# A third pair of K-blocks as seven products of sums in the feed-forward of a decoder layer

## Chip, cores and metric

The kernel runs on one core of a Trainium2 chip. The metric is the device time of one execution in microseconds (us), as the median of several runs. The program is one launch and every engine (TensorE, here PE; VectorE, DVE; ScalarE, ACT; GpSimd, POOL; SyncE, SP, which issues the weight loads) works through its own queue in order, with semaphores between them.

## The reference

One decoder layer over 256 tokens of width 2048, in float32: a norm, a token mixer with its input and output projections, a second norm, and a gated feed-forward with 5632 hidden columns. The part that matters here is this one:

```python
h = rms_norm(x, pre_ffn_g[l])
f = (jax.nn.silu(h @ w_gate[l]) * (h @ w_up[l])) @ w_down[l]
x = x + rms_norm(f, post_ffn_g[l])
```

## The kernel before

**Precision.** Each float32 operand is held as a rounded high part (hi) and the rest (lo), both in a 32-bit matmul type. A product is three matmuls into one PSUM bank: hi times hi, lo times hi, hi times lo (L664 to L666 in the joint chunks; the stationary side is a 128x128 block of activations, the moving side 128x512 weights). The weights come from memory in float32 as `raw` tiles of two K-blocks by 512 columns (512 KB). For a tile in plain use ACT makes hi (L79) and DVE makes lo = raw - hi (L81).

**Chunks.** The hidden columns are cut into 11 chunks of 512. Chunk 0 and chunks 9 and 10 are done gate first, then up. Chunks 1 to 8 (`gate_up`, L716) take gate and up together: the 16 K-blocks (128 rows each) are gone through as 8 pairs, p = 0 to 7. For one pair the operands are 2x2 blocks on both sides: two token blocks by two K-blocks of activations, and two K-blocks by two column chunks (gate, up) of weights.

**Two ways for a pair.** A plain pair ("P", `plain_pair`, L611) is eight products into four banks: four with the gate tile, then four with the up tile. A pair in `S_PAIRS` ("S", `seven_products`, L619) is seven products of sums into seven banks (Winograd's form): the sums of activation blocks are made once (`x1_sums`, L711, `token_sums`, L577); the sums of weight blocks are made anew for every chunk on DVE, in place in the raw tiles (L627 to L629 three, L635 one), and are split into hi (ACT, L623, L624, L634, L636) and lo (DVE, L605, four times). PE's order in an S pair is: two products with `h1`, one with `h22` (the tile `m`), two with `h3` (`hi_sb`), two with `h2` (`hi_sa`). Before the change S_PAIRS is (2, 5).

**After the last S pair** of a chunk (p = 5) one copy on ACT (L672) and four additions on DVE (L673 to L676) bring four of the seven banks together in `comb`. After pair 7 DVE adds the plain banks (L743 for gate, L750 for up), ACT takes the tanh (L745), DVE multiplies (L746, L695). The rows are transposed on PE (L687) at the end of pair 1 of the next chunk, and DVE and ACT take them out of PSUM (L690, L691).

**Buffers.** There are four raw tiles (`wraw`, L64), so the load for pair p+2 goes into a tile that pair p gives back. SP's queue issues the loads (L77 for plain pairs, L601 for S pairs), in order, two for each pair. There are five hi and five lo tiles (`wsplit`, L61); a plain pair takes two of each, an S pair three. `m22` (tag h9, one buffer) holds `h22` and `l22` of an S pair. The tag h10 (one buffer) holds the temporary of the activation sums, and later `comb`.

**Order.** The order of each engine's queue is not the source order: it is fixed when the program is put together, by what can run and by source order among that, and is the same in each execution. So work of one chunk and of the next stands mixed in DVE's and ACT's queues, as the rows below show.

Of the kernel before, what the change touches and what calls it, by code (L numbers as in the profile page):

```python
# [9 lines left out]
F32R = mybir.dt.float32r  # L10
# [4 lines left out]
P = 128  # L15
# [18 lines left out]
def trunk(  # L34
# [123 lines left out]
    with ExitStack() as mctx:  # L158
# [318 lines left out]
        x1_of = lambda kb: (x1_hi[:, kb], x1_lo[:, kb])  # L477
# [77 lines left out]
    hpool = ctx.enter_context(tc.tile_pool(name="hpool", bufs=1, side="right"))  # L555
    gctx = actx.enter_context(ExitStack())
    gu = gctx.enter_context(tc.tile_pool(name="gu", bufs=1))
# [17 lines left out]
    sums = {}  # L575

    def token_sums(key, pairs, hi, lo, tmp, home):  # L577

        n = pairs * 512
        a = tmp[:, 0].rearrange("p (q e t) -> p q e t", q=pairs, e=2)  # L580
        f = tmp[:, 1].rearrange("p (q s t) -> p q s t", q=pairs, s=4)
        nc.vector.tensor_tensor(out=tmp[:, 0].rearrange("p (k t) -> p k t", k=2 * pairs), in0=hi.bitcast(F32),
                                in1=lo.bitcast(F32), op=ALU.add)
        a11, a21 = a[:, :, 0, TB[0]], a[:, :, 0, TB[1]]
        a12, a22 = a[:, :, 1, TB[0]], a[:, :, 1, TB[1]]
        nc.vector.scalar_tensor_tensor(out=f[:, :, 0], in0=a21, scalar=-1.0, in1=a22, op0=ALU.mult, op1=ALU.subtract)
        nc.vector.scalar_tensor_tensor(out=f[:, :, 1], in0=f[:, :, 0], scalar=-1.0, in1=a11, op0=ALU.mult,
                                       op1=ALU.subtract)
        nc.vector.tensor_tensor(out=f[:, :, 2], in0=a11, in1=a21, op=ALU.subtract)
        nc.vector.tensor_tensor(out=f[:, :, 3], in0=a12, in1=f[:, :, 1], op=ALU.subtract)  # L590
        flat = tmp[:, 1]
        s_hi = home[:, 0].rearrange("p q s t -> p (q s t)")
        s_lo = home[:, 1].rearrange("p q s t -> p (q s t)")
        nc.scalar.copy(out=s_hi, in_=flat)
        nc.vector.tensor_tensor(out=s_lo, in0=flat, in1=s_hi.bitcast(F32), op=ALU.subtract)
        for q in range(pairs):
            sums[key, q] = [(home[:, 0, q, j], home[:, 1, q, j]) for j in range(4)]

    def fetch(piece):
        raw = wraw.tile([P, 2, 512], F32, tag="raw", name="raw")  # L600
        nc.sync.dma_start(out=raw, in_=piece)  # L601
        return raw

    def lo_of(lo, raw, hi):
        nc.vector.tensor_tensor(out=lo, in0=raw, in1=hi.bitcast(F32), op=ALU.subtract)  # L605

    def block(act_of, kb, tb):
        hi, lo = act_of(kb)
        return hi[:, TB[tb]], lo[:, TB[tb]]

    def plain_pair(srcs, p, act_of):  # L611

        out = []
        for src, banks in zip(srcs, ((1, 3), (2, 7))):
            hi, lo = split_weights(src[p], 2, 512)
            out.append([(banks[tb], block(act_of, 2 * p + e, tb), (hi[:, e], lo[:, e])) for e in range(2) for tb in range(NT)])
        return out

    def seven_products(srcs, p, act_of, s_of, h22, l22):  # L619
        ra, rb = (fetch(src[p]) for src in srcs)  # L620
        h1 = wsplit.tile([P, 2, 512], F32R, tag="hi", name="hi")
        l1 = wsplit.tile([P, 2, 512], F32R, tag="lo", name="lo")
        nc.scalar.copy(out=h1, in_=ra)  # L623
        nc.scalar.copy(out=h22, in_=rb[:, 1])  # L624
        lo_of(l1, ra, h1)
        lo_of(l22, rb[:, 1], h22)
        for out, in0, in1, op in ((ra[:, 0], ra[:, 0], rb[:, 0], ALU.subtract), (rb[:, 0], rb[:, 1], rb[:, 0], ALU.subtract),  # L627
                                  (rb[:, 1], rb[:, 1], ra[:, 0], ALU.add)):
            nc.vector.tensor_tensor(out=out, in0=in0, in1=in1, op=op)  # L629
        h2 = wsplit.tile([P, 2, 512], F32R, tag="hi", name="hi_sa")  # L630
        l2 = wsplit.tile([P, 2, 512], F32R, tag="lo", name="lo_sa")
        h3 = wsplit.tile([P, 2, 512], F32R, tag="hi", name="hi_sb")
        l3 = wsplit.tile([P, 2, 512], F32R, tag="lo", name="lo_sb")
        nc.scalar.copy(out=h3, in_=rb)  # L634
        nc.vector.tensor_tensor(out=ra[:, 1], in0=ra[:, 1], in1=rb[:, 1], op=ALU.subtract)  # L635
        nc.scalar.copy(out=h2, in_=ra)  # L636
        lo_of(l3, rb, h3)
        lo_of(l2, ra, h2)
        s1n, s2, s3, s4 = s_of
        return [[(0, block(act_of, 2 * p, 0), (h1[:, 0], l1[:, 0])),  # L640
                 (1, block(act_of, 2 * p + 1, 0), (h1[:, 1], l1[:, 1])),
                 (2, s4, (h22, l22))],
                [(6, s3, (h3[:, 0], l3[:, 0])),
                 (5, s2, (h3[:, 1], l3[:, 1]))],
                [(4, s1n, (h2[:, 0], l2[:, 0])),
                 (3, block(act_of, 2 * p + 1, 1), (h2[:, 1], l2[:, 1]))]]
# [3 lines left out]
    def products_into(kinds, new_bank):  # L650

        left = {}
        for k in kinds:
            for b, n in (PLAIN if k == "P" else tuple((b, 1) for b in range(7))):
                left[b] = left.get(b, 0) + n
        banks = {}

        def product(b, a, w):
            start = b not in banks
            if start:  # L660
                banks[b] = new_bank(b)
            left[b] -= 1
            (a_hi, a_lo), (w_hi, w_lo) = a, w
            nc.tensor.matmul(banks[b], lhsT=a_hi, rhs=w_hi, start=start, stop=False)  # L664
            nc.tensor.matmul(banks[b], lhsT=a_lo, rhs=w_hi, start=False, stop=False)  # L665
            nc.tensor.matmul(banks[b], lhsT=a_hi, rhs=w_lo, start=False, stop=left[b] == 0)  # L666

        return banks, product
# [11 lines left out]
    def bank_in(tags):  # L680
        return lambda b: POOL_OF[tags[b]].tile([P, 512], F32, tag=tags[b], name=f"bank{b}")
# [21 lines left out]
    def later_rows(c, aa, tag):  # L703
        yield
        hidden_rows(c, aa, tag)

    S_PAIRS = (2, 5)

    def x1_sums(p):  # L711
        tmp = hpool.tile([P, 2, 512], F32, tag="h10", name="sums_f")
        home = gu.tile([P, 2, 1, 4, P], F32R, tag=f"sums{p}", name=f"sums{p}")
        token_sums(("x1", p), 1, x1_hi[:, 2 * p:2 * p + 2], x1_lo[:, 2 * p:2 * p + 2], tmp, home)

    def gate_up(c, extra):  # L716
        odd = c % 2
        plain = ("acc",) * 4 if odd else ("tr", "mx", "tr", "mx")
        shared = ("mx", "tr", "tr", "mx") if odd else ("acc",) * 4
        tags = dict(zip((1, 2, 3, 7, 0, 4, 5, 6), plain + shared))  # L720
        kinds = ["S" if p in S_PAIRS else "P" for p in range(KB // 2)]
        banks, product = products_into(kinds, bank_in(tags))
        srcs = (w_gate[c], w_up[c])
        comb = None
        for p, k in enumerate(kinds):
            if p in extra:
                extra[p]()
            if k == "P":
                parts = plain_pair(srcs, p, x1_of)
            else:  # L730
                m22 = hpool.tile([P, 2, 512], F32R, tag="h9", name="m22")
                parts = seven_products(srcs, p, x1_of, sums[("x1", p), 0], m22[:, 0], m22[:, 1])
            for part in parts:
                for b, a, w in part:
                    product(b, a, w)
            advance()
            if p == S_PAIRS[-1]:
                comb = hpool.tile([P, 4, 512], F32, tag="h10", name="comb")
                partial_sums(banks, *(comb[:, i] for i in range(4)))
        aa = []  # L740
        for tb in range(NT):
            g = comb[:, 2 * tb]
            nc.vector.tensor_tensor(out=g, in0=g, in1=banks[(1, 3)[tb]], op=ALU.add)  # L743
            a = ft.tile([P, 512], F32, tag="fa", name="fa")
            nc.scalar.activation(out=a, in_=g, func=AF.Tanh, scale=hr2[:, tb:tb + 1])  # L745
            nc.vector.scalar_tensor_tensor(out=a, in0=a, scalar=1.0, in1=g, op0=ALU.add, op1=ALU.mult)  # L746
            aa.append(a)
        for tb in range(NT):
            u = comb[:, 2 * tb + 1]
            nc.vector.tensor_tensor(out=u, in0=u, in1=banks[(2, 7)[tb]], op=ALU.add)  # L750
        up_times(aa, [comb[:, 1], comb[:, 3]])
        pending.append(later_rows(c, aa, "acc" if odd else "tr"))

    pending.append(up_part(0, aa, up0))
    for c in range(1, 9):
        gate_up(c, {0: lambda: x1_sums(2), 3: lambda: x1_sums(5)} if c == 1 else {})
    for c in range(9, NCH):
        accs = matmul_chunk(w_gate[c], KB, 512, x1_of)
        aa = [gate_part(tb, accs[tb]) for tb in range(NT)]
# [204 lines left out]
```

## Time and profile before

| what | value |
|---|---|
| median of 3 runs | 1127.92 us (1127.82 to 1128.39) |
| the profiled execution's own time | 1127.93 us |
| its span, first to last instruction | 1126.2 us |
| mean granted TensorE clock | 0.997 of full |
| busy share of the span: PE, DVE, ACT | 99%, 73%, 51% |
| chunks 1 to 8 of the feed-forward | about 450 to 796 us from the span's start |

The span leaves out 1.7 us of the execution's own time, which is what lies ahead of the first and behind the last instruction. In the rows below, times are in us from the start of the span unless a column is said to be in ns, and L12 is line 12 of the kernel before. A matmul of 512 columns is shown with a modelled end and overlaps the next one; what one costs is read from the distance of starts.

### The profile page before, as it was taken

The page shows a single profiled execution, that of the slowest core. Times are in us where ns is not written, and L with a number is a line of the kernel's source. Part 1 is how long each engine was busy: PE and PEld are TensorE (multiplying, and loading weights), DVE is VectorE, ACT ScalarE, POOL GpSimd, SP SyncE. Part 2 cuts the span into 40 slices and gives each one's busy share as a digit, 9 for nine tenths or more (in the row PEclk, how much of TensorE's full clock was granted, in tenths as well). Part 3 has the DMA queues.
Part 4 walks back from the last instruction along what each step waited for, and adds up shares of the span by engine and source line. Part 5 has one row for each costly group of instructions (what it writes and reads, how often), then busy time and mean ns, then how long its engine had stood idle before and what let it go on. Part 6 is the DMA issues. An engine that isn't in the chain of part 4 may idle for free.

```text
span 1126.2 us, 14203 instructions
## 1 busy us (share of the span) xinstructions
PE 1113.6 (99%) x5198; PEld 937.4 (83%) x5198; DVE 817.0 (73%) x1039; ACT 578.4 (51%) x792; POOL 27.5 (2%) x55
## 2 busy tenths in 40 slices
PE   9999999999999999999999999999999999999996
PEld 7888899998888878888888888888888888888885
DVE  6655555656778488797888987888655787777775
ACT  7644445655644356455455545445444454554451
POOL 0000000000200001000000000000000000000000
PEclk9999999999999999999999999999999999999998
DMA  9855555566566547467457457556655456665662
GB/s 355 267 190 185 169 161 182 162 217 194 170 195 235 186 148 227 154 195 235 164 183 239 157 187 233 178 187 221 204 192 187 145 191 225 220 214 194 213 213 86
DMA packets 65014, 221.35 MB, mean 197 GB/s; under 512 B 7344, under 2 KB 9392, under 8 KB 64432
## 3 DMA queue, kind: packets, MB, share of 16 engines
q1 hardware_dynamic: 64656, 220.30, 59.8%
q8 instruction: 40, 0.66, 0.2%
q14 instruction: 30, 0.25, 0.1%
q10 hardware_dynamic: 288, 0.15, 0.1%
HBM read 218.32 MB, written 2.10 MB: 196 GB/s over the span
## 4 chain that ended last, share of the span: by engine, by line
PE 96%; DVE 2%; DMA 1%; issue 1%; ACT 0%; POOL 0%; POOLq 0%; DVEq 0%; ACTq 0%; SPq 0%
PE bank L666 16%; PE bank L664 16%; PE bank L665 16%; PE acc L88 15%; PE acc L90 14%; PE acc L89 14%; PE h_ps L687 1%; DMA raw<-in_w_down_dram 1%; PE qk_ps L235 0%; PE sc L267 0%; DMA cols<-in_cols_dram 0%; PE yt_ps L191 0%; DVE x_lo L499 0%; DVE lo L81 0%; PE o_ps L243 0%
## 5 line engine op out<-in xcount | busy, mean ns | idle before, releaser
L81 DVE TENSOR_TENSOR lo<-raw,hi 128x1024 fp32r<-128x1024 f32 (+2 forms) x353 | 415.8, 1184 | 233.8 <-ACT hi L79 224.2
L79 ACT CAST hi<-raw 128x1024 fp32r<-128x1024 f32 (+2 forms) x353 | 358.0, 1018 | 341.4 <-PE acc L89 148.4
L88 PE MATMUL acc<-hi,x_hi 128*128 128x512 f32 (+1 forms) x640 | 244.5, 382 | 0.7 <-ACT x_hi L183 0.7
L89 PE MATMUL acc<-hi,x_lo 128*128 128x512 f32 (+1 forms) x640 | 239.5, 374 | 0.0
L90 PE MATMUL acc<-lo,x_hi 128*128 128x512 f32 (+1 forms) x640 | 239.2, 375 | 0.0
L664 PE MATMUL bank<-hi,x_hi 128*128 128x512 f32 x416 | 162.5, 391 | 0.0
L666 PE MATMUL bank<-lo,x_hi 128*128 128x512 f32 x416 | 161.9, 389 | 0.0
L665 PE MATMUL bank<-hi,x_lo 128*128 128x512 f32 x416 | 161.8, 389 | 0.0
L88 PEld LDWEIGHTS acc<-hi,x_hi 128*128 128x128 f32 x640 | 120.6, 188 | 19.5 <-issue 2.0
L90 PEld LDWEIGHTS acc<-lo,x_hi 128*128 128x128 f32 x640 | 120.5, 188 | 18.3
L89 PEld LDWEIGHTS acc<-hi,x_lo 128*128 128x128 f32 x640 | 120.7, 189 | 17.0 <-DVE x_lo L184 0.2
L664 PE MATMUL bank<-hi,h 128*128 128x512 f32 x280 | 109.1, 390 | 0.0
L665 PE MATMUL bank<-hi,h 128*128 128x512 f32 x280 | 108.9, 389 | 0.0
L666 PE MATMUL bank<-lo,h 128*128 128x512 f32 x280 | 108.9, 389 | 0.0
L666 PEld LDWEIGHTS bank<-lo,x_hi 128*128 128x128 f32 x416 | 78.1, 188 | 16.3
L665 PEld LDWEIGHTS bank<-hi,x_lo 128*128 128x128 f32 x416 | 78.1, 188 | 16.0
L664 PEld LDWEIGHTS bank<-hi,x_hi 128*128 128x128 f32 x416 | 78.1, 188 | 15.9
L634 ACT CAST hi_sb<-raw 128x1024 fp32r<-128x1024 f32 x28 | 29.4, 1051 | 112.7 <-DVE raw L629 103.3
L664 PEld LDWEIGHTS bank<-hi,h 128*128 128x128 f32 x280 | 52.6, 188 | 11.1 <-DVE h L691 0.4
L666 PEld LDWEIGHTS bank<-lo,h 128*128 128x128 f32 x280 | 52.6, 188 | 10.9
L665 PEld LDWEIGHTS bank<-hi,h 128*128 128x128 f32 x280 | 52.6, 188 | 10.9
L629 DVE TENSOR_TENSOR raw<-raw 128x512 f32<-128x512 f32 x84 | 58.0, 690 | 1.9
(214 smaller groups left out, 1210.0 us busy)
## 6 DMA issues: line engine op xcount, KB each, us to landing
raw<-in_w_gate_dram SPq DMA_DIRECT2D x88, 512.0 KB, 4.3
raw<-in_w_up_dram SPq DMA_DIRECT2D x88, 512.0 KB, 4.5
raw<-in_w_down_dram SPq DMA_DIRECT2D x88, 512.0 KB, 4.4
raw<-in_w_ret_dram SPq DMA_DIRECT2D x47, 512.0 KB, 4.2
raw<-in_w_diff_dram SPq DMA_DIRECT2D x48, 384.0 KB, 3.2
raw<-in_w_out_dram SPq DMA_DIRECT2D x32, 512.0 KB, 3.6
raw<-in_w_sgu_dram SPq DMA_DIRECT2D x16, 512.0 KB, 3.9
x_sb<-in_x_dram SPq DMA_DIRECT2D x2, 1024.0 KB, 8.3
```

Source lines behind the costliest of these rows:

```text
L79: nc.scalar.copy(out=hi, in_=raw)
L81: nc.vector.tensor_tensor(out=lo, in0=raw, in1=hi.bitcast(F32), op=ALU.subtract)
L88: nc.tensor.matmul(ps, lhsT=a_hi, rhs=wh, start=first, stop=False)
L89: nc.tensor.matmul(ps, lhsT=a_lo, rhs=wh, start=False, stop=False)
L90: nc.tensor.matmul(ps, lhsT=a_hi, rhs=wl, start=False, stop=last)
L629: nc.vector.tensor_tensor(out=out, in0=in0, in1=in1, op=op)
L634: nc.scalar.copy(out=h3, in_=rb)
L664: nc.tensor.matmul(banks[b], lhsT=a_hi, rhs=w_hi, start=start, stop=False)
L665: nc.tensor.matmul(banks[b], lhsT=a_lo, rhs=w_hi, start=False, stop=False)
L666: nc.tensor.matmul(banks[b], lhsT=a_hi, rhs=w_lo, start=False, stop=left[b] == 0)
L687: nc.tensor.transpose(out=pt[:, i], in_=aa[tb][:, i * P:(i + 1) * P], identity=ident)
```

## The change

Pair 4 joins pairs 2 and 5 as an S pair in chunks 1 to 8. The list's new order (2, 5, 4) only serves to pick which sums get which home; pairs are still gone through as 0 to 7, so the kinds are now P P S P S S P P. The sums of the activation blocks of pair 4 are made in chunk 1, at pair 1. A tile of the tag h9, which was allocated anew for each S pair as `m22`, is allocated once: its first half holds the sums of pair 4, its second half `h22` and `l22` of whichever S pair is in work. The combination still follows pair 5.

```diff
-    S_PAIRS = (2, 5)
+    S_PAIRS = (2, 5, 4)
+
+    h9_tile = hpool.tile([P, 4, 512], F32R, tag="h9", name="m22_sums")
 
     def x1_sums(p):
         tmp = hpool.tile([P, 2, 512], F32, tag="h10", name="sums_f")
-        home = gu.tile([P, 2, 1, 4, P], F32R, tag=f"sums{p}", name=f"sums{p}")
+        if p in S_PAIRS[:2]:
+            home = gu.tile([P, 2, 1, 4, P], F32R, tag=f"sums{p}", name=f"sums{p}")
+        else:
+            home = h9_tile[:, 0:2].rearrange("p m (q s t) -> p m q s t", q=1, s=4)
         token_sums(("x1", p), 1, x1_hi[:, 2 * p:2 * p + 2], x1_lo[:, 2 * p:2 * p + 2], tmp, home)
...
             else:
-                m22 = hpool.tile([P, 2, 512], F32R, tag="h9", name="m22")
-                parts = seven_products(srcs, p, x1_of, sums[("x1", p), 0], m22[:, 0], m22[:, 1])
+                parts = seven_products(srcs, p, x1_of, sums[("x1", p), 0], h9_tile[:, 2], h9_tile[:, 3])
...
-            if p == S_PAIRS[-1]:
+            if p == max(S_PAIRS):
...
-        gate_up(c, {0: lambda: x1_sums(2), 3: lambda: x1_sums(5)} if c == 1 else {})
+        gate_up(c, {0: lambda: x1_sums(2), 1: lambda: x1_sums(4), 3: lambda: x1_sums(5)} if c == 1 else {})
```

## Rows read from the trace of the kernel before

**Rows 1.** The page: PE and DVE over the span, and the chain's shares.

```profile
PE 1113.6 (99%) x5198; PEld 937.4 (83%) x5198; DVE 817.0 (73%) x1039; ACT 578.4 (51%) x792; POOL 27.5 (2%) x55
...
PE 96%; DVE 2%; DMA 1%; issue 1%; ACT 0%; POOL 0%; POOLq 0%; DVEq 0%; ACTq 0%; SPq 0%
```

**Rows 2.** Busy us (instructions) in stretches: chunk 0's end; two joint chunks.

```profile
core 0: us, PE busy (x) PEld busy (x) DVE busy (x) ACT busy (x) POOL busy (x), PEclk, DMA share, GB/s
424.00:449.00 25.00, 25.00 (x112) 20.71 (x111) 19.95 (x29) 15.40 (x22) 2.90 (x4) 1.00 0.71 230
504.10:547.19 43.09, 43.09 (x197) 35.74 (x195) 36.66 (x43) 22.32 (x26) 0.00 (x0) 1.00 0.61 196
547.19:590.25 43.06, 43.06 (x196) 35.74 (x195) 36.66 (x43) 22.33 (x26) 0.00 (x0) 1.00 0.61 195
```

**Rows 3.** Timeline of PE in pairs 4 and 5: start, us, instruction.

```profile
517.10 0.39 PE L664 MATMUL bank<-hi,x_hi 128*128 128x512 f32 x1
...
517.78 0.39 PE L664 MATMUL bank<-hi,x_hi 128*128 128x512 f32 x1
...
522.99 0.39 PE L666 MATMUL bank<-lo_sb,sums 128*128 128x512 f32 x1
```

**Rows 4.** Timeline of DVE over one joint chunk: start, us, instruction, [idle before].

```profile
506.18 1.28 DVE L691 TENSOR_TENSOR h<-h_ps,h 128x512 fp32r<-128x512 f32 x2
507.38 1.22 DVE L81 TENSOR_TENSOR lo<-raw,hi 128x1024 fp32r<-128x1024 f32 x1
...
510.93 1.23 DVE L605 TENSOR_TENSOR lo<-raw,hi 128x1024 fp32r<-128x1024 f32 x1
512.07 0.68 DVE L605 TENSOR_TENSOR m<-raw,m 128x512 fp32r<-128x512 f32 x1
512.67 2.13 DVE L629 TENSOR_TENSOR raw<-raw 128x512 f32<-128x512 f32 x3
514.84 0.69 DVE L635 TENSOR_TENSOR raw<-raw 128x512 f32<-128x512 f32 x1
516.01 1.23 DVE L605 TENSOR_TENSOR lo_sb<-raw,hi_sb 128x1024 fp32r<-128x1024 f32 x1 [0.47 <-ACT hi_sb L634]
517.15 1.22 DVE L605 TENSOR_TENSOR lo_sa<-raw,hi_sa 128x1024 fp32r<-128x1024 f32 x1
...
523.03 1.23 DVE L81 TENSOR_TENSOR lo<-raw,hi 128x1024 fp32r<-128x1024 f32 x1 [0.21 <-ACT hi L79]
524.18 0.68 DVE L673 TENSOR_TENSOR comb<-comb,bank 128x512 f32<-128x512 f32 x1
...
526.70 0.68 DVE L675 TENSOR_TENSOR comb<-comb,bank 128x512 f32<-128x512 f32 x1
527.30 0.68 DVE L676 TENSOR_TENSOR comb<-comb,bank 128x512 f32<-128x512 f32 x1
...
536.82 1.28 DVE L750 TENSOR_TENSOR comb<-comb,bank 128x512 f32<-128x512 f32 x2
538.02 1.41 DVE L695 SCALAR_TENSOR_TENSOR fa<-fa,hrr,comb 128x512 f32<-128x512 f32 x2
539.34 1.22 DVE L605 TENSOR_TENSOR lo<-raw,hi 128x1024 fp32r<-128x1024 f32 x1
```

**Rows 5.** Waits, 504.1 to 590.25 us: who waited for whom, us, times, longest.

```profile
ACT hi L79 <- PE bank L665: 16.2, 14, 1.7
```

**Rows 6.** The same view over all joint chunks, 449.8 to 800 us.

```profile
DVE m L605 <- ACT m L624: 0.9, 1, 0.9
```

**Rows 7.** Reload of a raw tile: SP's queue, ACT's timeline, and median us to landing.

```profile
517.26 0.33 SPq L77 DMA_DIRECT2D raw<-in_w_gate_dram  x1
...
521.95 1.05 ACT L79 CAST hi<-raw 128x1024 fp32r<-128x1024 f32 x1
...
raw<-in_w_gate_dram SPq DMA_DIRECT2D x16, 512.0 KB, 4.5
```

**Rows 8.** Tile sums_f: duration in ns min/median/max, first and last start.

```profile
L586 DVE SCALAR_TENSOR_TENSOR sums_f<-sums_f x5: 286/419/423, 434.8 to 910.3; 128x256 f32<-128x256 f32 x3, 128x128 f32<-128x128 f32 x2
L582 DVE TENSOR_TENSOR sums_f<-x_hi,x_lo x2: 681/687/693, 427.2 to 437.5; 128x512 f32<-128x512 f32 x2
```

**Rows 9.** Timeline of PE: the start, and the longest later pause.

```profile
5.60 0.77 PE L88 MATMUL acc<-hi,x_hi 128*128 128x512 f32 x1 [0.72 <-ACT x_hi L183]
...
9.18 0.40 PE L90 MATMUL acc<-lo,x_hi 128*128 128x512 f32 x1
...
398.75 0.63 PE L496 MATMUL x_ps<-ident,hx 128*128 128x128 f32 x4 [0.47 <-issue]
```

## The prediction

> **What bounds the kernel now.** I began with the page: PE is busy 99% of the span and holds 96% of the chain that ended last [rows 1]. A busy PE may still be waiting on somebody's pace, so the second view was busy time in stretches, over single joint chunks. PE has no hole in them: a chunk lasts 43.07 us (mean of two), PE is busy all of it, DVE 36.66 us and ACT 22.3 us [rows 2]. A matmul product costs the distance of two product starts, 0.68 us [rows 3]. A chunk has 6 x 8 + 2 x 7 = 62 products, 42.2 us; the transposes fill the rest. So PE sets the pace, and DVE has 6.4 us of air in each chunk. The third view was the list of waits: the idle time of the other engines is mostly ACT waiting for PE to give back a hi tile (16.2 us in two chunks) [rows 5]. DVE and ACT run ahead of PE as far as their five hi and lo tiles allow. The lead in numbers: the last write to `lo_sb` of pair 5 ends at 516.01 + 1.23 = 517.24 [rows 4], PE first reads it at 522.99 [rows 3], 5.7 us later. This lead is what the change spends.
>
> **What PE saves.** Pair 4 has seven products instead of eight: 0.68 us in each of eight chunks, 5.4 us in all, and a PE-bound chunk of 42.39 us.
>
> **What DVE pays.** I take starts to starts, since neighbours on DVE overlap a little. A plain pair is two L81 of 1.14 us (516.01 to 517.15 for the same shape), 2.28 us. An S pair runs from 510.93 to 517.15 + 1.14 = 518.29, 7.36 us, of which 0.47 us is a wait for ACT inside the pair that recurs every time [rows 4]. The ends of a chunk (L673 to L676, L743, L746, L750, L691: twelve instructions of 0.60; L695 twice 0.66) are 7.2 + 1.3 = 8.5 us [rows 4]. Before: 2 x 7.36 + 6 x 2.28 + 8.5 = 36.9 us, which agrees with the busy row. After: 3 x 7.36 + 5 x 2.28 + 8.5 = 42.0 us. Against PE's 42.39 that leaves DVE 0.4 us of idle time in a chunk. Any gap beyond it that recurs in each chunk makes DVE the bound.
>
> By the Trainium skill, "VectorE: DVE Perf Modes", section on the DRAIN, the next operation does not start until the pipe of the one before has emptied, unless nothing holds it. Under that rule full durations would add up: with 1.22 us for each 1024-wide subtraction, my estimate for DVE is nearer 44 us a chunk, which would be over PE's without a single gap. The rows show the next start 0.08 us before the end, so I keep the 42.0.
>
> **Gaps that DVE cannot run around.** With four raw tiles, a tile's way round is: DVE frees it, SP issues the load, it lands, ACT makes hi, DVE makes lo. The load takes 4.5 us, issue to landing [rows 7]; ACT adds 1.08 us (521.95 to DVE's start at 523.03) [rows 4, 7]. From a release to the next lo on that tile 5.6 us must pass; the row pair 517.24 to 523.03 has 5.8. Today it is hidden by the lead. With pairs 4 and 5 both S, I follow DVE in its order:
> - After pair 5: its first tile is free 1.05 us before DVE's last start-to-start step ends, so pair 7 can begin 4.55 us after pair 5. In between stands pair 6, 2.28 us. Gap 2.27 us.
> - After pair 7: pair 1 of the next chunk needs pair 7's first tile, 1.23 + 5.6 = 6.83 us after pair 7 began; pairs 7 and 0 fill 4.56. Gap 2.27 us.
> - After pair 2: pair 4 begins 4.55 us after; pair 3 and L691 fill 2.28 + 1.2. Gap 1.07 us.
>
> The four additions L673 to L676 (2.4 us) can fill one of the first two gaps, and L743 with L746 up to half of the other, if the queue has them there and PE has finished those banks. In the queue of before they stand behind a plain L81 (523.03, then 524.18) [rows 4], so I don't count on both. The bounds of DVE's idle time: 2.0 us (both filled but for 0.9, and 1.07) and 5.6 us (none filled). A DVE-bound chunk is then 44.0 to 47.6 us. I take one gap filled and a little of the rest: 3.8 us, a chunk of 45.8 us.
>
> **The sum.** Chunk 1 begins with the whole lead of 5.7 us and spends it: taken as even. Seven chunks at 45.8 - 43.07 = +2.7 us give +19.1 us; after chunk 8 plain pairs follow and no more is lost. The ends: 7 x 0.9 = +6.5 and 7 x 4.5 = +31.7. Sums are made against the profiled execution (1127.93 us, span 1126.2), which lies 0.01 us from the median, so both give **1147 us**, and 1134 to 1160 as this case's own range.
>
> **Smaller edits.** The sums of pair 4 are once 0.69 + 4 x 0.29 + 0.69 us on DVE (the last is L595, taken as L582's like) [rows 8], 2.5 us; before, such sums start at 427 and 437 us in chunk 0, where DVE is idle 5 of 25 us [rows 2]: nothing, and 2.5 us if they come in chunk 1. ACT gains a half-width and a full-width cast, some 1.6 us on 22.3: nothing. The loads are the same in number and size. The one tile for `h22` and `l22` makes pair 5's write wait for PE's third product of pair 4, only one pair back instead of three. The nearest row is a wait of DVE for `m`, 0.9 us, once in all joint chunks [rows 6]; from nothing to 0.9 us a chunk, I take nothing, because PE runs close behind DVE's pair 4 and DVE has L629 steps to do meanwhile; 7 x 0.9 = 6.3 us is kept for the upper end.
>
> **Rivals.**
> - **PE stays the bound.** 42.0 against 42.39: if the queue's order fills all three gaps, the chunk falls to 42.39 us and the time to 1127.9 - 5.4 = 1122.5 us. For it speaks that DVE's work still fits; against it that three gaps of 5.6 us must shrink to 0.4. It decides at that point: idle time of DVE under 0.4 us in a chunk. The Trainium skill, "Perfetto Trace Analysis", section on the most-contended engine, would have the engine with the highest occupancy optimized, and calls Vector's occupancy a fair measure of its limit. By that rule PE's saving is gained, as DVE at 42.0 of 42.39 is still the less occupied. Chance 0.11.
> - **It comes out even.** Gaps of about 1.1 us a chunk: DVE takes 43.1, and the time stays at 1126 to 1130 us. Chance 0.06.
> - **Pauses cost PE its clock.** Holes of 1 to 3 us will appear on PE. After the start PE's first eight 512-wide matmuls take 9.18 - 5.60 = 3.58 us, the level of 1.2 GHz; at today's 0.2275 us they would take 1.82. A later pause of 0.47 us changed nothing (clock 1.00 in the joint chunks) [rows 2, 9]; longer ones don't occur. One fall in each of seven chunks is 7 x 1.76 = 12 us on top of 1147: 1159 us, and 1172 with all gaps open. The Trainium skill, "TensorE: Matmul & The Clock Gate", Part 1, says that idleness brings the slow clock back; no row here shows it after the start. Chance 0.15, with other mishaps of the queue's order.
> - **The forecast** has what is left, 0.68.
>
> **How the numbers follow.** A difference of 0.2% (2.3 us) is about what can be told from no change here. Faster 0.11, same 0.06, slower 0.83. The range goes from 1129 (all of the forecast's case and the upper part of even) to 1167 (the forecast's upper end plus the wait for `m`); outside it lie the faster case, most of even and the far end of the clock case, under 0.2.
>
> **What would show it.** In the changed trace, DVE should be busy about 41 us of each joint chunk of 44 to 47.6, PE should show holes at `hi_sb` or `lo_sb` products of pairs 4 and 5 and at bank uses behind L691, ACT's waits for PE should shrink, and SP's waits for L605 grow. A joint chunk of 42.4 us with a gapless PE proves me wrong; so would DVE busy well under 41 us with PE waiting on something else than DVE.

## The result, and the profile after

After the change the kernel takes 1138.34 us (median of 4 runs, 1137.74 to 1140.8) against 1128.04 us for the kernel before on the same chip (4 runs, 1127.82 to 1128.39). The ratio is 1.0095 [1.0083, 1.0108]: slower by 10.3 us. The forecast was slower, 1147 us, in a range of 1129 to 1167.

The profiled execution of after took 1138.82 us (span 1137.1). Its page, in the lines that answer to [rows 1]:

```profile
PE 1114.1 (98%) x5174; PEld 929.9 (82%) x5174; DVE 852.3 (75%) x1093; ACT 588.7 (52%) x809; POOL 27.4 (2%) x55
...
PE 73%; DVE 13%; DMA 6%; issue 4%; ACT 3%; POOL 0%; SPq 0%; DVEq 0%; POOLq 0%; ACTq 0%
```

PE issues 24 matmuls fewer, which is eight products of three matmuls. Yet its share of the chain that ended last falls from 96% to 73%: DVE, ACT and the weight transfers now stand in it.

Busy time in stretches of after, cut where the transposes (L687) of a chunk start (the first two joint chunks, then the next five), in the columns of [rows 2]:

```profile
461.27:547.97 86.70, 85.70 (x383) 70.12 (x382) 78.16 (x93) 45.22 (x53) 0.00 (x0) 1.00 0.56 186
547.97:771.78 223.81, 216.76 (x956) 174.64 (x955) 204.45 (x241) 118.04 (x136) 0.00 (x0) 1.00 0.57 188
```

The same stretches of before:

```profile
460.89:547.03 86.14, 86.14 (x390) 71.48 (x389) 72.51 (x84) 44.44 (x50) 0.00 (x0) 1.00 0.58 188
547.03:762.36 215.33, 215.33 (x971) 178.69 (x970) 183.12 (x211) 111.48 (x125) 0.00 (x0) 1.00 0.61 196
```

The first two chunks lose only 0.56 us together. The next five lose 8.48 us: 44.76 us each instead of 43.07. PE has 7.05 us of holes in them, where before had none. It lost more than that, because the modelled end of a matmul covers the first part of each hole: where two matmuls start 0.92 us apart instead of 0.23 (611.64 and 612.56), the trace shows a hole of about 0.5. The granted clock stays at 1.00.

Where PE waits in after, over the first seven joint chunks (what waited <- for whom: us in total, times, longest us):

```profile
PE bank L666 <- DVE lo_sb L605: 3.2, 6, 0.5
PE bank L664 <- ACT hi_sb L634: 2.7, 6, 1.3
PE bank L664 <- DVE h L691: 2.2, 6, 0.6
```

These are the forecast's three places: `hi_sb` and `lo_sb` of S pairs, and a bank behind L691. The waits of all engines, over four of the later chunks:

```profile
ACT hi_sb L634 <- DVE raw L629: 50.0, 12, 6.3
ACT hi L79 <- DMA raw<-in_w_up_dram: 11.6, 11, 1.9
ACT hi L79 <- DMA raw<-in_w_gate_dram: 9.5, 11, 1.5
ACT m_sums L624 <- DMA raw<-in_w_up_dram: 6.4, 5, 2.7
DVE lo_sb L605 <- ACT hi_sb L634: 5.7, 13, 0.5
DVE lo L81 <- ACT hi L79: 5.1, 9, 1.7
...
DVE m_sums L605 <- ACT m_sums L624: 3.4, 4, 2.1
```

The first line, ACT's wait for DVE's weight sums, is 4.2 us for each S pair; before it was 4.7 (18.7 us for four S pairs, 504.1 to 590.25 us). The change is in the other lines: ACT no longer waits for PE to give back a hi tile, as it did [rows 5]. It waits for loads, and DVE waits for ACT. Last, SP's queue over the same four chunks:

```profile
SPq L77 <- DVE lo_sb L605: 47.0, 8, 5.9
SPq L601 <- DVE lo_sb L605: 35.7, 4, 9.2
```

These waits for `lo_sb` are 82.7 us; in four chunks of before (547.19 to 719.47 us) they are 62.1. So a circle has closed: DVE frees a raw tile, SP loads it, ACT splits it, DVE goes on. The timeline of DVE in one chunk of after (587.35 to 631.67 us) shows it:

```profile
587.35 1.22 DVE L605 TENSOR_TENSOR lo<-raw,hi 128x1024 fp32r<-128x1024 f32 x1
...
594.70 1.22 DVE L81 TENSOR_TENSOR lo<-raw,hi 128x1024 fp32r<-128x1024 f32 x1
595.83 1.28 DVE L691 TENSOR_TENSOR h<-h_ps,h 128x512 fp32r<-128x512 f32 x2
597.03 1.22 DVE L81 TENSOR_TENSOR lo<-raw,hi 128x1024 fp32r<-128x1024 f32 x1
598.51 1.23 DVE L605 TENSOR_TENSOR lo<-raw,hi 128x1024 fp32r<-128x1024 f32 x1 [0.26 <-ACT hi L623]
599.94 0.69 DVE L605 TENSOR_TENSOR m_sums<-raw,m_sums 128x512 fp32r<-128x512 f32 x1 [0.20 <-ACT m_sums L624]
...
608.75 0.69 DVE L605 TENSOR_TENSOR m_sums<-raw,m_sums 128x512 fp32r<-128x512 f32 x1
...
611.28 1.23 DVE L605 TENSOR_TENSOR lo_sb<-raw,hi_sb 128x1024 fp32r<-128x1024 f32 x1 [0.39 <-ACT hi_sb L634]
612.42 1.22 DVE L605 TENSOR_TENSOR lo_sa<-raw,hi_sa 128x1024 fp32r<-128x1024 f32 x1
613.66 1.23 DVE L81 TENSOR_TENSOR lo<-raw,hi 128x1024 fp32r<-128x1024 f32 x1
614.80 0.68 DVE L673 TENSOR_TENSOR comb<-comb,bank 128x512 f32<-128x512 f32 x1
615.40 1.22 DVE L81 TENSOR_TENSOR lo<-raw,hi 128x1024 fp32r<-128x1024 f32 x1
616.53 0.68 DVE L674 TENSOR_TENSOR comb<-comb,bank 128x512 f32<-128x512 f32 x1
617.19 1.23 DVE L81 TENSOR_TENSOR lo<-raw,hi 128x1024 fp32r<-128x1024 f32 x1
...
624.13 1.23 DVE L81 TENSOR_TENSOR lo<-raw,hi 128x1024 fp32r<-128x1024 f32 x1 [0.52 <-ACT hi L79]
...
631.67 1.22 DVE L605 TENSOR_TENSOR lo<-raw,hi 128x1024 fp32r<-128x1024 f32 x1
```

How to read it: pair 5's first raw tile is last read by the `lo_sb` subtraction, which ends at 611.28 + 1.23 = 612.51. Pair 7 needs that tile; its first lo starts at 617.19, 4.7 us later. Pair 6 (613.66, 615.40) and two additions happen to fill that gap. Pair 7's own first tile is free at 617.19 + 1.23 = 618.42, and the next chunk's pair 1 gets it at 624.13, 5.7 us later, which the work in between does not quite fill. Pair 2's first tile comes back as pair 4's at 598.51, with waits of 0.26 and 0.20 us there. Counting starts to starts as the prediction did, these gaps leave DVE idle for 2.3 us of the 44.32. The remaining 42.0 us are its work, with the short wait inside each S pair that the prediction counted in.

### The profile page after: what moved, and what is told of

Same layout as the page of the kernel before. It is cut to its first block, busy times and chain, and to the rows that moved or that the text cites. A ratio compares the mean times of both kernels' runs of the same rounds, so it can differ in the third digit from the quotient of the medians.

```text
span 1137.1 us, 14242 instructions
## 1 busy us (share of the span) xinstructions
PE 1114.1 (98%) x5174; PEld 929.9 (82%) x5174; DVE 852.3 (75%) x1093; ACT 588.7 (52%) x809; POOL 27.4 (2%) x55
## 4 chain that ended last, share of the span: by engine, by line
PE 73%; DVE 13%; DMA 6%; issue 4%; ACT 3%; POOL 0%; SPq 0%; DVEq 0%; POOLq 0%; ACTq 0%
PE acc L88 14%; PE acc L90 14%; PE acc L89 14%; PE bank L666 9%; PE bank L664 9%; PE bank L665 9%; DMA raw<-in_w_up_dram 4%; DVE raw L629 3%; DMA raw<-in_w_gate_dram 2%; DVE lo L81 2%; ACT hi_sb L634 2%; DVE lo L605 1%; DVE lo_sa L605 1%; DVE m_sums L605 1%; DVE lo_sb L605 1%
## 5 line engine op out<-in xcount | busy, mean ns | idle before, releaser
L81 DVE TENSOR_TENSOR lo<-raw,hi 128x1024 fp32r<-128x1024 f32 (+2 forms) x337 | 396.4, 1182 | 201.9 <-ACT hi L79 191.8
L79 ACT CAST hi<-raw 128x1024 fp32r<-128x1024 f32 (+2 forms) x337 | 339.3, 1015 | 300.3 <-PE acc L89 151.1
L664 PE MATMUL bank<-hi,x_hi 128*128 128x512 f32 x368 | 143.9, 391 | 0.0
L666 PE MATMUL bank<-lo,x_hi 128*128 128x512 f32 x368 | 143.3, 389 | 0.0
L665 PE MATMUL bank<-hi,x_lo 128*128 128x512 f32 x368 | 143.2, 389 | 0.0
L90 PEld LDWEIGHTS acc<-lo,x_hi 128*128 128x128 f32 x640 | 120.1, 188 | 18.7 <-DVE lo L81 0.8
L634 ACT CAST hi_sb<-raw 128x1024 fp32r<-128x1024 f32 x36 | 37.8, 1050 | 137.1 <-DVE raw L629 131.3
L666 PEld LDWEIGHTS bank<-lo,x_hi 128*128 128x128 f32 x368 | 69.1, 188 | 14.5
L665 PEld LDWEIGHTS bank<-hi,x_lo 128*128 128x128 f32 x368 | 69.1, 188 | 14.1
L664 PEld LDWEIGHTS bank<-hi,x_hi 128*128 128x128 f32 x368 | 69.1, 188 | 14.0
L629 DVE TENSOR_TENSOR raw<-raw 128x512 f32<-128x512 f32 x108 | 74.6, 691 | 2.6
```

The source lines that it names most:

```text
L79: nc.scalar.copy(out=hi, in_=raw)
L90: nc.tensor.matmul(ps, lhsT=a_hi, rhs=wl, start=False, stop=last)
```

## The experiments

The theory under test (reload): DVE's work of 42.0 us would fit under PE's 42.39, and the loss is the way round through only four raw tiles, three times a chunk. Its rivals: the one tile for `h22` and `l22` (shared tile); DVE has simply too much to do (sheer work); the short waits inside each S pair for ACT's cast `hi_sb` (in-pair waits); PE's clock. Line numbers in the kernels with a new helper argument are one higher (L606 is L605 of after, L82 is L81).

**1. Pair 7's raw tiles out of the ring.** `plain_pair` and `split_weights` take raw tiles from outside, and pair 7 has two of its own (in SBUF that lies free in these chunks). In the ring the next pair 0 then follows pair 5 at a distance of two pairs:

```diff
-    def split_weights(src, kbs, width):
-        raw = wraw.tile([P, kbs, width], F32, tag="raw", name="raw")
+    def split_weights(src, kbs, width, raw=None):
+        if raw is None:
+            raw = wraw.tile([P, kbs, width], F32, tag="raw", name="raw")
...
-                parts = plain_pair(srcs, p, x1_of)
+                raws = (None, None)
+                if p == 7:
+                    r2 = hpool.tile([P, 2, 2, 512], F32, tag="h8", name="raw_h8")
+                    raws = (r2[:, 0], r2[:, 1])
+                parts = plain_pair(srcs, p, x1_of, raws)
```

> The changed kernel, with the two loads of pair 7 of each joint chunk in a tile of their own instead of the ring of four raw tiles. Reload theory (DVE sets the pace, and half of its excess is idle time in which it waits for a raw tile that was freed too late): the gaps after pair 5 and after pair 7 close, the chunk falls from 44.85 us to 42.5 to 43.0 us, the time from 1138.3 to 1122 to 1127 us. Theory of DVE's sheer work (its instructions alone fill the chunk): nothing changes, 1136 to 1140 us. Theory of the shared tile for h22 (pair 5 waits for PE's third product of pair 4): nothing changes either.

Measured: 1128.11 us (11 runs, 1126.46 to 1130.66) against 1128.17; ratio 1.000 [0.9991, 1.0009]. No DVE operation is touched (in its queue only L691 moves, behind the second subtraction of pair 3; run 9 has that order too, and no gain), and 10.2 of the 10.3 us are back: most of the loss is the ring. It is still 1 us over the expected range. What DVE waits for in four of its chunks (546 to 717 us):

```profile
DVE lo_sb L606 <- ACT hi_sb L635: 5.3, 12, 0.5
DVE m_sums L606 <- ACT m_sums L625: 2.1, 3, 0.9
DVE m_sums L606 <- PE bank L667: 0.5, 1, 0.5
```

The gaps behind pairs 5 and 7 are gone. Left are the waits for `m_sums`, ahead of pair 4 (the third gap), and those inside pairs. Runs 9 and 12 tell these apart.

**2. The three S pairs spread out.** Is it that pairs 4 and 5 are neighbours? (The activation sums of pairs 1 and 3 are then made in place of those of 2 and 4; that line is left out here.)

```diff
-    S_PAIRS = (2, 5, 4)
+    S_PAIRS = (1, 5, 3)
```

> The changed kernel with the three pairs at 1, 3 and 5 instead of 2, 4 and 5, so that no two stand together. Reload theory: pairs 3 and 5 must then reload the tiles of pairs 1 and 3 with only one plain pair of 2.28 us in between, one gap of about 2.3 us more in each chunk: 46 to 48 us a chunk, 1147 to 1162 us. Theory that two adjacent pairs collide: 42.4 to 43.5 us a chunk, 1122 to 1130 us. Theory of sheer work: 1136 to 1140 us.

Measured: 1153.82 us (4 runs, 1149.93 to 1155.62); ratio 1.0222 [1.0204, 1.0239], inside the reload theory's range. Spread out is worse, as the ring says: now one plain pair lies between two S pairs twice in a chunk, and each S pair waits for the tile of the one before. DVE over the end of one S pair and the start of the next:

```profile
653.45 1.23 DVE L605 TENSOR_TENSOR lo_sb<-raw,hi_sb 128x1024 fp32r<-128x1024 f32 x1 [0.46 <-ACT hi_sb L634]
...
655.73 2.36 DVE L81 TENSOR_TENSOR lo<-raw,hi 128x1024 fp32r<-128x1024 f32 x2
659.28 1.23 DVE L605 TENSOR_TENSOR lo<-raw,hi 128x1024 fp32r<-128x1024 f32 x1 [1.19 <-ACT hi L623]
661.09 0.69 DVE L605 TENSOR_TENSOR m_sums<-raw,m_sums 128x512 fp32r<-128x512 f32 x1 [0.59 <-ACT m_sums L624]
```

The first tile is free at 653.45 + 1.23 = 654.68, and its next lo starts at 659.28, 4.6 us later. A plain pair of 2.36 us is all that DVE has in between, besides one more subtraction of the S pair.

**3. A tile of its own for pair 4's `h22` and `l22`.**

```diff
-                parts = seven_products(srcs, p, x1_of, sums[("x1", p), 0], h9_tile[:, 2], h9_tile[:, 3])
+                m22 = h9_tile[:, 2:4] if p != 4 else hpool.tile([P, 2, 512], F32R, tag="h8", name="m22b")
+                parts = seven_products(srcs, p, x1_of, sums[("x1", p), 0], m22[:, 0], m22[:, 1])
```

> The changed kernel with a tile of its own for h22 and l22 of pair 4, so that pair 5 need not wait for PE's third product of pair 4. Reload theory and sheer work: nothing changes, 1136 to 1140 us. Theory of the shared tile: DVE's wait of about 0.9 us a chunk for this tile goes, 1130 to 1133 us.

Measured: 1136.97 us (5 runs, 1134.69 to 1137.75); ratio 1.0072 [1.0059, 1.0085]. The shared tile is worth at most 1.4 us of the 10.3 at the medians (the order of DVE's queue differs here too), taking it at nothing was close, and the rival falls. The trace of after says why: ACT's cast into the tile does wait for PE (it starts at 606.23, 0.24 us after the last matmul of PE's third product of pair 4 at 605.99, and so in seven of the eight chunks). But the cast takes 0.62 us, and when DVE comes to `m_sums`, at 608.75 in the timeline above, it has no wait for it.

**4. Pair 4's weight sums left out** (`no_sums` is true for p = 4; its three L629 additions and its L635 are missing):

```diff
+            if no_sums:
+                break
...
-        nc.vector.tensor_tensor(out=ra[:, 1], in0=ra[:, 1], in1=rb[:, 1], op=ALU.subtract)
+        if not no_sums:
+            nc.vector.tensor_tensor(out=ra[:, 1], in0=ra[:, 1], in1=rb[:, 1], op=ALU.subtract)
```

> The changed kernel without the four weight additions of pair 4 (three of L629 and the L635 there are left out, so the sums of that pair are not formed; PE, ACT and the loads do the same work). DVE's work falls by 4 x 0.72 = 2.9 us a chunk, from 42.0 to 39.1. Both theories in which DVE sets the pace: the chunk falls to PE's 42.4 us, 1120 to 1125 us, and this is what the change would give if DVE's part were free. Theory of the shared tile: 1136 to 1140 us.

Measured: 1124.42 us (5 runs, 1122.91 to 1124.75); ratio 0.9963 [0.995, 0.9975]. By itself this separates nothing: less work on DVE and an earlier release both come from it. It shows that PE's saving is there to be had: 13.9 us under after.

**5. and 6. A dose of DVE work,** four additions of 0.6 us a chunk that read `comb`, behind L754, once in after and once in before:

```diff
+        idle = hpool.tile([P, 512], F32, tag="h8", name="idle")
+        for _ in range(4):
+            nc.vector.tensor_tensor(out=idle, in0=comb[:, 1], in1=comb[:, 3], op=ALU.add)
```

> The changed kernel with four more 512-wide additions on DVE in each joint chunk (into a scratch tile, behind L754), 4 x 0.60 = 2.4 us. If DVE sets the pace and has no idle time at that place, the chunk grows by 2.4 us and the time by 7 to 8 times that: 1154 to 1158 us. If PE or a load set the pace, up to 1141 us.

> The kernel before with the same four additions in each joint chunk. It has 6.4 us of idle DVE a chunk and a lead of 5.7 us: no change, 1127 to 1130 us, if air on DVE is what separates the two kernels. If DVE's work itself slowed PE (by its memory traffic, say), 2 us or more slower, as in the changed kernel.

Measured in after: 1158.46 us (4 runs, 1157.34 to 1159.39), ratio 1.0265 [1.0249, 1.0281], 20.1 us over after and just above the expected range. Eight doses are 19.2 us, and the seven chunks after the first, which can pay, 16.8; what the rest is was not told apart (the order of DVE's queue and PE's clock changed too, as the last section shows). Measured in before: 1130.91 us (7 runs, 1129.75 to 1131.68), ratio 1.0023 [1.0013, 1.0034], 2.9 us, where nothing was expected: a small miss. There PE's weight loads wait for L691 (2.8 us in six chunks), which stands behind more work in DVE's queue. The same work costs before a seventh of what it costs after. That DVE paces after is shown; why it does so is not told by these two.

**7. and 8. Work from DVE to POOL,** on top of run 1: the multiplication L695 in one (its scale goes to ACT), L635 in the other.

```diff
-        up_times(aa, [comb[:, 1], comb[:, 3]])
+        for tb in range(NT):
+            nc.gpsimd.tensor_tensor(out=aa[tb], in0=aa[tb], in1=comb[:, 2 * tb + 1], op=ALU.mult)
+            nc.scalar.activation(out=aa[tb], in_=aa[tb], func=AF.Copy, scale=hrr[:, tb:tb + 1])
```

> The kernel with pair 7's own raw tile, and the last multiplication of a joint chunk (L695, two instructions, 1.3 us of DVE) done on POOL, with its scale on ACT. DVE's work falls under PE's 42.4 us a chunk: 1122 to 1125 us, faster than both kernels, if DVE's work is what still binds at 42.9 us. If POOL's reads hold DVE up, or something else than DVE binds there, 1127 to 1130 us.

```diff
-        nc.vector.tensor_tensor(out=ra[:, 1], in0=ra[:, 1], in1=rb[:, 1], op=ALU.subtract)
+        (eng or nc.vector).tensor_tensor(out=ra[:, 1], in0=ra[:, 1], in1=rb[:, 1], op=ALU.subtract)
```

> The kernel with pair 7's own raw tile, and the fourth weight addition of each of the three pairs (L635, 0.7 us of DVE each, 2.2 us a chunk) done on POOL in the joint chunks. It runs beside DVE, but ACT's h2 waits for it: if POOL's addition takes under about 2 us, 1122 to 1125 us; if it takes longer, h2 and its lo come late and the time is 1126 us or more.

Both missed: 1132.12 us (5 runs, 1131.2 to 1132.81; ratio 1.0033 [1.002, 1.0046]) and 1134.58 us (5 runs, 1134.44 to 1136.58; ratio 1.006 [1.0047, 1.0072]), 4.0 and 6.5 us behind run 1. DVE in the first of them, at the only stretch of the chunk in which POOL multiplies (624.59 to 628.12 us, two of 1.78 us in the mean):

```profile
623.77 1.27 DVE L759 TENSOR_TENSOR comb<-comb,bank 128x512 f32<-128x512 f32 x2
624.97 2.01 DVE L606 TENSOR_TENSOR lo<-raw,hi 128x1024 fp32r<-128x1024 f32 x1
626.90 1.78 DVE L606 TENSOR_TENSOR m_sums<-raw,m_sums 128x512 fp32r<-128x512 f32 x1
```

The same two subtractions take 1.22 and 0.69 us in run 1: DVE gives up 1.3 us of work and loses 1.9. In the second, the addition takes 1.29 us on POOL, and DVE's longest wait for `hi_sb` grows from 0.5 to 1.2 us.

**9. The cast of `hi_sb` in two halves,** against the in-pair waits; alone on after:

```diff
-        nc.scalar.copy(out=h3, in_=rb)
+        for e in range(2):
+            nc.scalar.copy(out=h3[:, e], in_=rb[:, e])
```

> The changed kernel with the halved cast of h3 alone. If DVE's own chain sets the pace, its three waits of 0.47 us come off each chunk: 7 to 8 times 1.4 us, 1127 to 1129 us. If the reload of the raw tiles is a chain of its own, part of it comes back there as waiting for loads: 1129 to 1135 us.

Measured: 1140.9 us (4 runs, 1138.91 to 1141.64), ratio 1.0108 [1.0094, 1.0122]: a miss for both theories. The in-pair waits did vanish, and nothing came of it. DVE's waits in five of its chunks (550 to 774 us):

```profile
DVE m_sums L605 <- ACT m_sums L624: 9.6, 10, 1.6
DVE lo L81 <- ACT hi L79: 7.2, 13, 1.7
```

ACT's order changed too: the cast of pair 5's `m_sums` now stands behind a half of `hi_sb` that waits for a DVE sum. So DVE waits for other casts, and PE for bank uses behind DVE. Run 10 has the same wait for `m_sums` with the longer ring (5.6 us in four chunks, longest 1.6), so that wait comes from ACT's order and not from the ring. What this run shows is only that taking the in-pair waits away does not bring the time back.

**10. Pairs 3 and 7 out of the ring, and the halved cast.** The two tiles of run 1 serve both pairs, so that pair 4 gets the tiles of pair 1 instead of pair 2's. **11.** The same two edits on before.

```diff
+                if p in (3, 7):
```

> The changed kernel with two edits that cost DVE nothing: pairs 3 and 7 of each joint chunk load into a tile of their own, and ACT casts h3 of an S pair in two halves, the first as soon as its half of the sum is there, so that DVE's wait of 0.47 us for it in each S pair goes. DVE then needs 42.9 - 1.4 - 0.5 = about 41.0 us a chunk, less than PE's 42.4: if DVE's work and its waits are all that took the gain away, PE sets the pace again and the time is 1121 to 1124 us, faster than both kernels. If the three S pairs cost something else too, 1126 us or more.

> The kernel before with the same two edits as the run with both. There PE sets the pace with 6.4 us of idle DVE a chunk, so nothing is gained: 1127 to 1129 us. If the edits gain by something else than DVE's air, 1122 to 1125 us.

Measured on after: 1123.34 us (5 runs, 1123.12 to 1123.86), ratio 0.9957 [0.9943, 0.9971], faster than both kernels. On before: 1128.62 us (11 runs, 1127.55 to 1129.57), ratio 1.0002 [0.9993, 1.0011]. The edits are worth nothing without the change, since PE has no hole there to close.

**12. Pairs 3 and 7 out of the ring, and nothing else,** on after.

> The changed kernel with pairs 3 and 7 on a tile of their own, without the halved cast. The run with pair 7 alone gave 1128.1 us, with both edits 1123.3. If the waits inside the pairs are what was left (DVE 42.9 us a chunk), this one stays at 1126 to 1128.5 us; if it was the reload ahead of pair 4 (0.5 to 0.9 us of waiting for m a chunk), it is at 1122.5 to 1125.5 us and the halved cast adds little.

Measured: 1122.85 us (5 runs, 1122.49 to 1123.92) against 1128.18; ratio 0.9953 [0.994, 0.9967]. This is the lowest median, level with run 10's 1123.34. Its page's PE and DVE, and two of its chunks:

```profile
PE 1108.2 (99%) x5174; PEld 933.0 (83%) x5174; DVE 849.5 (76%) x1093; ACT 587.9 (52%) x809; POOL 27.4 (2%) x55
```

```profile
545.30:587.70 42.40, 42.40 (x192) 35.17 (x192) 40.55 (x49) 23.44 (x27) 0.00 (x0) 1.00 0.57 199
587.70:630.10 42.40, 42.40 (x192) 35.19 (x192) 40.48 (x49) 23.47 (x27) 0.00 (x0) 1.00 0.58 199
```

A chunk is 42.40 us, PE without a hole, as the prediction has it for a PE-bound chunk (42.39). DVE's waits (546 to 717 us):

```profile
DVE lo_sb L606 <- ACT hi_sb L635: 5.3, 12, 0.5
DVE m_sums L606 <- ACT m_sums L625: 0.7, 3, 0.3
```

The in-pair waits stand as in run 1, to the tenth, and cost nothing. What went is the wait ahead of pair 4. DVE does the same operations as in after, in the order of run 1: 15.5 us, the distance from after (1138.34) to here, are the ring of raw tiles, about 10.2 of them behind pairs 5 and 7 (run 1) and 5.3 ahead of pair 4.

## Why the prediction was right, step by step

- **PE's saving** (5.4 us, chunk of 42.39): exact. Run 12 lies 5.3 us under before, with chunks of 42.40.
- **DVE's work** (36.9, then 42.0 us) is borne out: the steps of the chunk shown add up to 44.32 less 2.33 of gaps, and run 12 fits the same operations into 42.40. Full durations added up would not have fitted: those of run 12's 48 operations in a chunk are 43.2 us without any wait. The overlap of 0.08 us in the rows decides. The Trainium skill, "VectorE: DVE Perf Modes", section on the DRAIN, which the prediction weighed, exempts an operation that nothing holds; the overlap in the trace agrees.
- **The gaps** were the right cause, at the right three places. The size was off: idle time was taken at 3.8 us and came out at 44.76 - 42.0 = 2.8, within the bounds of 2.0 to 5.6. So the forecast's loss of 19.1 us is nearly twice the measured 10.3: its direction was reasoned, its size was loose. The term that was off is the reload of 5.6 us from release to lo, taken for all three. It was 4.7 us behind pair 5 (its load landed in 3.6 us instead of 4.5), 5.7 behind pair 7, and 4.9 ahead of pair 4 (593.65 to 598.51). Besides, the additions L673 to L676 went two and two into the first two gaps, so that the first was closed whole.
- **The lead**: the forecast let it carry the first chunk, and that is about what it did. But 5.7 us was never there to be carried over. With pair 4 an S pair, DVE has 7.36 - 2.28 = 5.1 us more to do just ahead of pair 5. In chunk 1 of after, `lo_sb` of pair 5 is finished at 477.61 + 1.23 = 478.84, only 0.8 us ahead of PE's first read, and PE's first hole comes in chunk 2:

```profile
477.61 1.23 DVE L605 TENSOR_TENSOR lo_sb<-raw,hi_sb 128x1024 fp32r<-128x1024 f32 x1 [0.39 <-ACT hi_sb L634]
```

```profile
479.61 0.39 PE L666 MATMUL bank<-lo_sb,sums 128*128 128x512 f32 x1
...
507.63 0.50 PE L664 MATMUL bank<-hi_sb,sums 128*128 128x512 f32 x1 [0.18 <-DVE h L691]
```

  In run 12, where PE has no hole, the lead at this place is 0.8 us in every chunk: most of it is spent and won back inside each chunk. Measured from transposes to transposes, the first chunk gains 0.7 us (42.37 against 43.05), the second loses 1.3, then five lose 1.7 each, and the last stretch 1.3 (38.99 against 37.65), together 10.4 us.
- **Smaller edits**: pair 4's activation sums ran in chunk 0, at nothing. The shared tile, taken at nothing with 6.3 us kept for the upper end, cost at most 1.4 us in all.
- **Rivals**: PE stays the bound was wrong for this kernel and came true in run 12: DVE's work fits under PE's, and the ring kept it from doing so. It comes out even wanted gaps of 1.1 us a chunk; they were 2.8. The clock rival did not occur in after: PE's longest wait in the list above was 1.3 us and the clock stayed at 1.00. By the Trainium skill, "Perfetto Trace Analysis", Optimization Strategy, a gap that repeats on the engine that should be saturated can mean too few buffers. The trace agrees: PE's holes repeat in each chunk, and two more raw tiles took 15.5 us off.
- **A reading that was not right**: in the two chunks of [rows 5], the prediction puts the idle time of the other engines mostly down to ACT waiting for PE to give back a hi tile (16.2 us). The same view has more for ACT waiting for DVE's weight sums (18.7 us). No term of the sum hangs on it.

What stays open: how much of run 3's 1.4 us is the shared tile's, what run 5 pays beyond its own additions, and whether runs 7 and 8 would gain something from run 12's buffers; none of these was tried.

## What to carry to other kernels

When work is moved to an engine that has air, compare not only its busy sum with the new bound but follow each buffer once round: release, load, cast, use. DVE, busy 41 of 44.8 us, was the bound of a loop whose ring was too short. Work added to it was paid in full (run 5), and two more buffers gave back more (run 12, 15.5 us) than four operations a chunk taken off it (run 4, 13.9 us). Read a lead at the place where the new work lands: what that work takes within one turn of the loop is no reserve for the turns after.

## What the runs showed of the hardware that was not expected

**POOL slows DVE.** While POOL multiplied two SBUF tiles, DVE's subtractions of two SBUF tiles took 2.01 us instead of 1.22, and 1.78 instead of 0.69 (run 7, and within 0.03 us the same in six more of its chunks). The Trainium skill, "SBUF — State Buffer", Who interferes with whom, says that a DVE instruction with two SBUF inputs contends with a GpSimd instruction that reads SBUF; the trace agrees.

**Holes of about 2.2 us on PE mostly brought half the clock; holes up to 1.7 us did not.** In run 5 the busy times around such a hole (2.16 us, 617.26 to 619.42):

```profile
617.00:619.40 2.40, 0.26 (x2) 0.00 (x0) 1.95 (x3) 1.08 (x2) 0.00 (x0) 1.00 0.41 164
619.40:620.40 1.00, 0.98 (x4) 0.70 (x5) 1.00 (x1) 1.00 (x2) 0.00 (x0) 1.00 0.00 0
620.40:624.00 3.60, 3.60 (x10) 2.88 (x10) 2.88 (x4) 1.81 (x2) 0.00 (x0) 0.53 0.60 182
624.00:630.00 6.00, 6.00 (x28) 4.95 (x27) 5.57 (x8) 3.15 (x3) 0.00 (x0) 1.00 0.79 270
```

The granted clock is 0.53 in the third row, the level of 1.2 GHz, from about 1 us after PE has resumed, and 1.00 before and behind it; ten matmuls stand in these 3.6 us instead of some sixteen. The Trainium skill, "TensorE: Matmul & The Clock Gate", Part 1, says that idleness brings the slow clock back, and the trace agrees. It did not do so each time. In the joint chunks of all runs the clock fell behind seven of eight holes of 2.16 to 2.21 us (five in run 5, one each in runs 2 and 9; a sixth in run 5, up to 812.13 us, changed nothing). It fell behind one of four of 1.95 to 2.00 us (runs 2 and 3), and behind none that was shorter. What it costs here is not told apart: PE was waiting for DVE anyway, but at 622.48 us DVE then waits 0.72 us for PE, which it does not do at that place in after.
